# The start of a hybrid encoder layer: first weights on another queue, the first block of x in two transfers, norm_w turned in between, three fillers fewer

## The chip, the cores and the metric

The kernel runs on one core of a Trainium2 chip. Its time is that of the device in microseconds. Three runs of the kernel before took 625.95, 626.0 and 626.17 us; the median is 626.0. The engines are named as in the profile: PE is TensorE (PEld its weight loads), ACT is ScalarE, DVE is VectorE, POOL is GpSimd, SP is SyncE, which here only issues transfers.

## The reference

One layer of a bidirectional encoder on 512 tokens of width 2048, all float32:

```
h     = rms_norm(x, norm_w)                       # norm_w has 2048 gains
proj  = h @ w_in                                  # w_in: 2048 x 4608
q, k, v, g_attn, xr, g_lru = split(proj)
attn  = softmax attention of q, k, v (8 heads, 2 for k and v, rope, q and k normed)
lru   = convolution of xr, then a gated linear recurrence forwards and backwards
mixed = [rms_norm(attn) * silu(g_attn), rms_norm(lru) * silu(g_lru)]
out   = x + mixed @ w_out                         # w_out: 2048 x 2048
```

## The kernel before

Nearly all of its time is matmul work on PE. Each float32 operand is split into a high part, rounded to the matmul's own 32-bit format, and a low part, what is left; a product is three matmuls: high by high, high by low and low by high (lines 153 to 155). The pieces are 128 x 128 against 128 x 512.

**The start.** The first product is x times the columns of w_in that make xr, from column C_XR = 2560, 512 columns at a time, accumulated over 16 row blocks of 128 (8 chunks of two). It needs x turned, features on partitions and tokens along the free axis. So for each block of 128 features four 128 x 128 tiles, one for each 128 tokens, are transposed by PE (`xturn`, line 258) into one PSUM bank. ScalarE scales the bank by that block's column of norm_w and writes the high part (line 263); VectorE writes the low part (line 266). norm_w itself arrives as 16 rows of 128 (the tile nw_st) and is also turned by PE, in `columns` (line 194), and copied to SBUF by VectorE (line 196). The weights arrive in the tile wr; for the first chunk VectorE casts the high part (line 223) and subtracts for the low part (line 224); later ScalarE casts. The first real matmul, of `proj_feat` at line 394, needs the high part of x's first block and of the first weights. The order on PE at that place is: high by high for the four pieces of the first weights, then the turns of x's second block, then the low parts.

**Fillers.** `busy(n)` (line 1167) issues n matmuls of a tile of ones into a bank that nobody reads. WARM = 12 of them stand ahead of everything on PE, WARM2 = 5 behind the turns of the first block.

**What sets the order.** At the start PE, ScalarE, VectorE and SyncE run in the order in which the code is written; each engine is in order, and waits on semaphores. A transfer is issued by SyncE's or ScalarE's queue and bumps one of eight completion semaphores, taken in turn over both queues (DMAHW0 to DMAHW7 in the order below); a transfer whose semaphore is still in use first waits for that earlier transfer. Before: norm_w goes out on ScalarE's queue, ahead of its table load (line 1184); SyncE issues x's first 128 features (256 KB, all tokens), the first 128 rows of weights (256 KB), x's second 128 features, the second weights, and then chunks of 512 KB, at lines 245 and 211.

**The last stage.** The output product reads blocks of w_out through `feed1` and `feed2`. In `feed2` the two halves of a block are fetched as one transfer, but for the second half of the columns (g = 1) and i < 3 as two (line 1004).

Of the kernel before, what the change touches and what calls it, by code (L numbers as in the profile page):

```python
# [11 lines left out]
F32 = mybir.dt.float32  # L12
# [5 lines left out]
P = 128  # L18
SEQ = 512
DM = 2048  # L20
KT = DM // P
NT = SEQ // P
# [17 lines left out]
SOON = 150  # L40


WARM, WARM2 = 12, 5


BEGIN, STEPS, LATE = 11, 2, 3
# [10 lines left out]
C_Q, C_K, C_GA, C_XR, C_GL = 0, 1024, 1536, 2560, 3584  # L57
# [6 lines left out]
def hybrid_kernel(  # L64
# [20 lines left out]
    nc = tc.nc  # L85
    xf = x.rearrange("b s d -> (b s) d")
# [5 lines left out]
    def opened(name, side):  # L92
        pools[name] = tc.alloc_tile_pool(name=name, bufs=1, side=side, reuse_waits="tile")
        order[side].append(name)
        return pools[name]
# [9 lines left out]
    wring = opened("wr", "left").ring(3 * 4096, name="wring")  # L105
# [12 lines left out]
    def nm(s):  # L118
        cnt[0] += 1
        return f"{s}_{cnt[0]}"  # L120

    def x2():
        return pools["xw"].tile([P, SEQ], F32R, tag="x2", bufs=32, name=nm("x2"))
# [4 lines left out]
    def b4(dt=F32, shape=(P, 2, SEQ)):  # L128
        return pools["lru"].tile(list(shape), dt, tag="b4", bufs=LRU_B4, name=nm("b4"))
# [13 lines left out]
    def mm():  # L143
        return ps.tile([P, SEQ], F32, tag="mm", name=nm("mm"))

    def const(shape, name, dt=F32):
        return cp.tile(list(shape), dt, tag=name, name=name)

    def f(ap):
        return ap.bitcast(F32)  # L150
# [21 lines left out]
    nw_st = const([KT, P], "nw_st")  # L172
# [14 lines left out]
    nw = const([P, KT], "nw")  # L187
    vec = const([P, R_END], "vec")

    def columns(dst, src):  # L190

        n = src.shape[0]
        pt = mm()
        nc.tensor.transpose(pt[:, :n], src, ident[:n, :n])  # L194
        with tc.high_priority():
            nc.vector.tensor_copy(dst, pt[:, :n])
# [6 lines left out]
    loads_done = {}  # L203

    def wraw(w, r0, c0, nk=1, queue=nc.sync):

        raw = wring.tile([P, 2, SEQ], F32, name=nm("wr"))
        src = w[r0 : r0 + 2 * P, c0 : c0 + SEQ].rearrange("(k p) e -> p k e", p=P)
        for k in range(nk):
            ks = slice(k * 2 // nk, (k + 1) * 2 // nk)  # L210
            loads_done[queue] = queue.dma_start(raw[:, ks, :], src[:, ks, :]).ins
            yield raw
# [3 lines left out]
    def wsplit(raw, k, copy=nc.scalar.copy):  # L216

        turn_of[0] += k
        pool = pools["wx" if "wx" in pools and turn_of[0] % 2 else "xw"]
        hi = pool.tile([P, SEQ], F32R, tag="wh", bufs=4, name=nm("wh"))  # L220
        lo = pool.tile([P, SEQ], F32R, tag="wl", bufs=4, name=nm("wl"))
        done = (
            copy(hi, raw[:, k, :]).ins,  # L223
            nc.vector.tensor_sub(lo, raw[:, k, :], f(hi)).ins,  # L224
        )
        split_done[-1] = split_done[turn_of[0] - k] = done
        return hi, lo
# [11 lines left out]
    def xload(c, nk=1):  # L239

        xc = b4(shape=(P, NT, 2 * P))
        for k in range(nk):
            ks = slice(k * 2 * P // nk, (k + 1) * 2 * P // nk)
            cs = slice(c * 2 * P + ks.start, c * 2 * P + ks.stop)
            nc.sync.dma_start(xc[:, :, ks], xf[:, cs].rearrange("(t p) d -> p t d", p=P))
            yield xc

    def behind(those):
        stack = ExitStack()
        for ins in those:  # L250
            stack.enter_context(tc.issue_after(ins))
        return stack

    def xturn(xc, kk, then=None):
        pt = mm()
        for t in range(NT):
            ks = slice(kk % 2 * P, (kk % 2 + 1) * P)
            nc.tensor.transpose(pt[:, t * P : (t + 1) * P], xc[:, t, ks], ident)  # L258
        if then:
            then()  # L260
        xh[kk], xl[kk] = x2(), x2()
        with behind(split_done[-1] if kk > 3 else ()):
            highs[kk // 2] = nc.scalar.activation(
                xh[kk], pt, AF.Identity, scale=nw[:, kk : kk + 1]
            ).ins
        nc.vector.scalar_tensor_tensor(
            xl[kk], pt, nw[:, kk : kk + 1], f(xh[kk]), op0=ALU.mult, op1=ALU.subtract
        )
# [39 lines left out]
    def xchunk(c):  # L308
# [3 lines left out]
        if c < TURNED:  # L312
            with tc.high_priority(AHEAD):
                for k in range(2):
                    xturn(xc, 2 * c + k)
            if c == 2:
                yield
            with behind(split_done[2][1:] if c == 2 else ()):
                xsquare(xc, c)
            yield  # L320
            return
# [555 lines left out]
    def split(*blocks):  # L877

        i = split_of[0] % 4
        split_of[0] += 1  # L880
        hi, lo = (
            pools["out" if i else "fin"].tile([P, 2, SEQ], F32R, tag=f"{t}{i}", bufs=1, name=nm(t))
            for t in ("wh", "wl")
        )
        n = 0
        for b in blocks:
            to = slice(n, n + b.shape[1])
            nc.scalar.copy(hi[:, to], b)  # L888
            nc.vector.tensor_sub(lo[:, to], b, f(hi[:, to]))  # L889
            n += b.shape[1]  # L890
        return hi, lo
# [9 lines left out]
    def block(m, k, c, n=1):  # L901

        return w_out[(2 * m + k) * P : (2 * m + k + 1) * P, c * SEQ : (c + n) * SEQ]
# [41 lines left out]
    def in_wr(n=2):  # L945
        return wring.tile([P, n, SEQ], F32, name=nm("wr"))

    def in_av(n=2):
        return aring.tile([P, n, SEQ], F32, name=nm("wr"))
# [48 lines left out]
    def feed2(g, i, got):  # L998

        m = mixed[i][0] // (2 * P)  # L1000
        x_ = in_wr()
        if g and i < 3:
            for j in range(2):
                nc.sync.dma_start(x_[:, j], block(m, 1, 2 * g + j))
        else:
            nc.sync.dma_start(x_.rearrange("p j e -> p (j e)"), block(m, 1, 2 * g, 2))
        if g == 0:
            z = in_av(1)
            nc.sync.dma_start(z[:, 0], t4[m])
        else:  # L1010
            z = kept_t2.pop(i)
            nc.vector.tensor_add(z, z, x_[:, 1:2])
        yield
        got.append(split(x_))
        yield
        got.append(split(z))
        yield

    def outputs(work):
# [6 lines left out]
        for g, n, i in order:  # L1026
            parts.append([])
            feeds.append((feed1, feed2)[n](g, i, parts[-1]))
# [136 lines left out]
    def busy(n):  # L1165
        for _ in range(n):
            nc.tensor.matmul(warm[:, : 2 * P], wv[:, :P], wv, start=True, stop=True)  # L1167
# [8 lines left out]
    )  # L1176
    given = {}
    with tc.high_priority():
        xs, ws = xload(0, 2), wraw(w_in, 0, C_XR, 2)
        nc.scalar.dma_start(nw_st, norm_w.rearrange("(k p) -> k p", p=P))  # L1180
        xc, raw = next(xs), next(ws)
        next(xs), next(ws)
        table = const([P, 1], "table")
        nc.scalar.activation(table, ones[:, :1], AF.Exp)
        first = []

        def split_first():
            first.append(wsplit(raw, 0, nc.vector.tensor_copy))

        columns(nw, nw_st)  # L1190
        xturn(xc, 0, split_first)
        busy(WARM2)
    stats = xstats()
# [29 lines left out]
    for step in proj_feat(C_XR, a1, first, given):  # L1223
        if step is None:
            with tc.high_priority():
                first.append(wsplit(raw, 1, nc.vector.tensor_copy))
                xturn(xc, 1)
            xsquare(xc, 0)
            move(None)
            given[1] = wload(w_in, 2 * P, C_XR)  # L1230
            continue
        c, e = step
        move(step)
        if (c, e) == (1, 2):
            s2.close()
        if (c, e) == (4, 2):
            with tc.high_priority(AHEAD):
                vec_load()
        if (c, e) == (7, 1):
            columns(vec, vec_st)  # L1240
        if (c, e) in ((4, 3), (KT // 2 - 1, 0)):
            with tc.high_priority(AHEAD), tc.issue_after(split_done[-1][1]):
                next(stats)
# [216 lines left out]
```

## Time and profile before

| | |
|---|---|
| median of three runs | 626.0 us (625.95 to 626.17) |
| the profiled execution | 626.48 us |
| its span, first to last instruction | 624.7 us |
| PE busy | 620.0 us, 99% of the span |
| DVE busy | 495.3 us, 79% |
| ACT busy | 352.4 us, 56% |
| POOL busy | 101.8 us, 16% |
| moved by transfers | 127.61 MB, 204 GB/s on average |

All times below are from the start of the span. Busy time of PE is modelled as overlapping: a matmul's length reaches over the start of the next one, so its rate is read from the distance of starts. The time around the span, 626.48 - 624.7 = 1.78 us, is not in the trace.

### The profile page before, as it was taken

How to read it: one execution, taken by the hardware profiler on the slowest of the kernel's cores; microseconds unless marked ns; L12 is line 12 of the kernel's file. 1: busy time of each engine (PE TensorE's matmuls, PEld its weight loads, DVE VectorE, ACT ScalarE, POOL GpSimd, SP SyncE). 2: the span in 40 equal slices, each digit the busy share in tenths (PEclk: the TensorE clock that was granted, in tenths of full speed). 3: DMA queues.
4: the chain of work that ended last, by engine and by line, in shares of the span. 5: the costliest groups of instructions: out<-in, count | busy, mean ns of one | idle time of the engine just before them, and what ended most of it. 6: DMA issues, size and time to landing. Idle time of an engine off the chain costs nothing.

```text
span 624.7 us, 8293 instructions
## 1 busy us (share of the span) xinstructions
PE 620.0 (99%) x2756; PEld 512.6 (82%) x2756; DVE 495.3 (79%) x800; ACT 352.4 (56%) x617; POOL 101.8 (16%) x135
## 2 busy tenths in 40 slices
PE   9999999999999999999999999999999999999997
PEld 7888888888888888888888888888888888888886
DVE  5958979986699876887887888549979866887776
ACT  3675799479946833545485548338345633443441
POOL 0000210112003622622123223100210101010010
PEclk9999999999999999999999999999999999999999
DMA  8878686759774599479659646932995777897252
GB/s 285 277 210 271 178 202 171 175 135 195 239 235 137 170 247 240 100 204 270 192 173 258 201 137 192 256 91 76 283 254 184 216 250 242 288 333 230 68 202 101
DMA packets 74026, 127.61 MB, mean 204 GB/s; under 512 B 6664, under 2 KB 29312, under 8 KB 73984
## 3 DMA queue, kind: packets, MB, share of 16 engines
q1 hardware_dynamic: 66096, 109.65, 56.7%
q0 software_dynamic: 7712, 17.31, 14.3%
q8 instruction: 21, 0.34, 0.2%
q14 instruction: 21, 0.17, 0.1%
q10 hardware_dynamic: 176, 0.14, 0.1%
HBM read 110.29 MB, written 37.75 MB: 237 GB/s over the span
## 4 chain that ended last, share of the span: by engine, by line
PE 99%; DVE 0%; issue 0%
PE pj L154 20%; PE pj L155 20%; PE pj L153 20%; PE mm L1040 14%; PE pj L1040 11%; PE mm L155 4%; PE mm L154 3%; PE mm L153 3%; PE pj L394 2%; PE mm L258 1%; PE mm L1167 1%; PE mm L836 0%; DVE cb L1069 0%; PE mm L194 0%; PE mm L373 0%; DVE ones L159 0%
## 5 line engine op out<-in xcount | busy, mean ns | idle before, releaser
L153 PE MATMUL pj<-x,wh 128*128 128x512 f32 x368 | 143.5, 390 | 0.0
L155 PE MATMUL pj<-x,wl 128*128 128x512 f32 x368 | 143.2, 389 | 0.0
L154 PE MATMUL pj<-x,wh 128*128 128x512 f32 x368 | 143.2, 389 | 0.0
L223 ACT CAST wh<-wr 128x512 fp32r<-128x512 f32 x142 | 84.5, 618 | 81.5 <-PE pj L154 29.8
L224 DVE TENSOR_TENSOR wl<-wr,wh 128x512 fp32r<-128x512 f32 x144 | 98.5, 712 | 20.5 <-ACT wh L223 19.2
L888 ACT CAST wh<-wr 128x1024 fp32r<-128x1024 f32 (+1 forms) x72 | 60.6, 860 | 75.3 <-PE mm L1040 36.0
L889 DVE TENSOR_TENSOR wl<-wr,wh 128x1024 fp32r<-128x1024 f32 (+1 forms) x72 | 68.6, 983 | 29.0 <-ACT wh L888 28.9
L153 PEld LDWEIGHTS pj<-x,wh 128*128 128x128 f32 x368 | 69.1, 188 | 14.4
L154 PEld LDWEIGHTS pj<-x,wh 128*128 128x128 f32 x368 | 69.1, 188 | 14.3
L155 PEld LDWEIGHTS pj<-x,wl 128*128 128x128 f32 x368 | 69.1, 188 | 14.3
L154 PE MATMUL pj<-wl,x 128*128 128x512 f32 x192 | 74.7, 389 | 0.0
L155 PE MATMUL pj<-wh,x 128*128 128x512 f32 x192 | 74.7, 389 | 0.0
L153 PE MATMUL pj<-wh,x 128*128 128x512 f32 x192 | 74.7, 389 | 0.0
L912 POOL DMA_DIRECT2D t<-in_w_out_dram x40 | 33.6, 907 | 156.0 <-DMA t<-in_w_out_dram 96.9
L1040 PE MATMUL mm<-wh,ml 128*128 128x512 f32 x126 | 49.0, 389 | 0.0
L1040 PE MATMUL mm<-wh,mh 128*128 128x512 f32 x126 | 49.0, 389 | 0.0
L1040 PE MATMUL mm<-wl,mh 128*128 128x512 f32 x126 | 49.0, 389 | 0.0
L153 PEld LDWEIGHTS pj<-wh,x 128*128 128x128 f32 x192 | 36.0, 188 | 7.6
L154 PEld LDWEIGHTS pj<-wl,x 128*128 128x128 f32 x192 | 36.0, 188 | 7.5
L155 PEld LDWEIGHTS pj<-wh,x 128*128 128x128 f32 x192 | 36.0, 188 | 7.4
L712 POOL TENSOR_SCALAR p<-p,sm 128x512 f32<-128x512 f32 x32 | 24.2, 761 | 89.4 <-DVE sm L711 89.4
L1040 PE MATMUL pj<-wl,mh 128*128 128x512 f32 (+1 forms) x100 | 38.5, 385 | 0.0
(205 smaller groups left out, 1052.9 us busy)
## 6 DMA issues: line engine op xcount, KB each, us to landing
wr<-in_w_in_dram SPq DMA_DIRECT2D x71, 512.0 KB, 5.0
wr<-in_w_out_dram SPq DMA_DIRECT2D x21, 512.0 KB, 5.1
t<-in_w_out_dram POOLq DMA_DIRECT2D x40, 256.0 KB, 7.1
wr<-t SPq DMA_DIRECT2D x40, 256.0 KB, 5.8
pd<-u SPq DMA_DIRECT2D x16, 512.0 KB, 3.0
pt<-pd SPq DMA_DIRECT2D x64, 128.0 KB, 4.1
t<-in_w_out_dram SPq DMA_DIRECT2D x24, 256.0 KB, 5.3
wr<-in_w_out_dram SPq DMA_DIRECT2D x22, 256.0 KB, 4.2
```

Source lines behind the costliest of these rows:

```text
L153: nc.tensor.matmul(acc, lh, rh, start=start, stop=False)
L154: nc.tensor.matmul(acc, lh, rl, start=False, stop=False)
L155: nc.tensor.matmul(acc, ll, rh, start=False, stop=stop)
L223: copy(hi, raw[:, k, :]).ins,
L224: nc.vector.tensor_sub(lo, raw[:, k, :], f(hi)).ins,
L258: nc.tensor.transpose(pt[:, t * P : (t + 1) * P], xc[:, t, ks], ident)
L394: nc.tensor.matmul(acc[e], w[:, e * P : (e + 1) * P], x_[2 * c + k], start=c == k == j == 0, stop=False,)
L712: last_pool[0] = nc.gpsimd.tensor_scalar(p, p, sm, 0.0, op0=ALU.mult, op1=ALU.add).ins
L888: nc.scalar.copy(hi[:, to], b)
L889: nc.vector.tensor_sub(lo[:, to], b, f(hi[:, to]))
L912: nc.gpsimd.dma_start(dst, src, accum_op=ALU.add)
L1040: nc.tensor.matmul(dst[s][:, es], lh[:, ts_], rh[:, es], start=i == ends_[0] and j == 0, stop=i == ends_[1] and j == 2,)
```

## The change

Five edits, four of them in the first 6 us:

- The first weights (256 KB) go out on ScalarE's queue, ahead of norm_w. SyncE issues x's first 128 features as two transfers of 128 KB, tokens 0 to 255 and 256 to 511, then x's second 128 features and the second weights.
- PE turns the first two token tiles of x, then norm_w, then the other two, instead of norm_w first.
- WARM goes from 12 to 11.
- WARM2 goes from 5 to 3.
- In `feed2` only i < 2 keeps two transfers, so one pair in the last stage becomes one transfer.

```diff
-WARM, WARM2 = 12, 5
+WARM, WARM2 = 11, 3
@@ xturn
         for t in range(NT):
+            if kk == 0 and t == 2:
+                columns(nw, nw_st)
             ks = slice(kk % 2 * P, (kk % 2 + 1) * P)
             nc.tensor.transpose(pt[:, t * P : (t + 1) * P], xc[:, t, ks], ident)
@@ feed2
-        if g and i < 3:
+        if g and i < 2:
@@ the start
     with tc.high_priority():
-        xs, ws = xload(0, 2), wraw(w_in, 0, C_XR, 2)
+        raw = wring.tile([P, 2, SEQ], F32, name=nm("wr"))
+        xc = b4(shape=(P, NT, 2 * P))
+        ws = w_in[: 2 * P, C_XR : C_XR + SEQ].rearrange("(k p) e -> p k e", p=P)
+        xs = xf[:, : 2 * P].rearrange("(t p) d -> p t d", p=P)
+        nc.scalar.dma_start(raw[:, 0], ws[:, 0])
+        for ts_ in (slice(0, 2), slice(2, 4)):
+            nc.sync.dma_start(xc[:, ts_, :P], xs[:, ts_, :P])
         nc.scalar.dma_start(nw_st, norm_w.rearrange("(k p) -> k p", p=P))
-        xc, raw = next(xs), next(ws)
-        next(xs), next(ws)
+        nc.sync.dma_start(xc[:, :, P:], xs[:, :, P:])
+        loads_done[nc.sync] = nc.sync.dma_start(raw[:, 1], ws[:, 1]).ins
         table = const([P, 1], "table")
         nc.scalar.activation(table, ones[:, :1], AF.Exp)
...
-        columns(nw, nw_st)
         xturn(xc, 0, split_first)
         busy(WARM2)
```

On PE, from the last filler of the first group to the first ones of the second, the order before (b is the block of x, nw_st the rows of norm_w, mm a PSUM bank; in brackets what a row waits for):

```order
L1167 MATMUL mm_115<-ones 128x256
L194 MATMUL mm_144<-ident,nw_st 128x16 [waits DMAHW0_49,Pool_49]
L258 MATMUL mm_147<-ident,b_2_136 128x128 [waits DMAHW1_49]
L258 MATMUL mm_147<-ident,b_2_136 128x128 x3
L1167 LDWEIGHTS ones
L1167 MATMUL mm_115<-ones 128x256
```

And now:

```order
L1169 MATMUL mm_115<-ones 128x256
L260 MATMUL mm_144<-ident,b_3_135 128x128 [waits DMAHW1_49,Pool_49]
L260 MATMUL mm_144<-ident,b_3_135 128x128
L194 MATMUL mm_147<-ident,nw_st 128x16 [waits DMAHW3_49]
L260 MATMUL mm_144<-ident,b_3_135 128x128 [waits DMAHW2_49]
L260 MATMUL mm_144<-ident,b_3_135 128x128
L1169 LDWEIGHTS ones
L1169 MATMUL mm_115<-ones 128x256
```

The turn of norm_w stands between the second and third turn of x, and three transfers are waited for in turn where there were two.

On SP, the head of the queue before (b is x, wr the weights; the 4x256 and 2x512 rows are the next chunks):

```order
L245 DMA b_2_136<-in_x_dram 128x4x128
L211 DMA wr_138<-in_w_in_dram 128x512
L245 DMA b_2_136<-in_x_dram 128x4x128
L211 DMA wr_138<-in_w_in_dram 128x512
L245 DMA b_19_190<-in_x_dram 128x4x256
L211 DMA wr_192<-in_w_in_dram 128x2x512
L245 DMA b_31_250<-in_x_dram 128x4x256
L245 DMA b_38_282<-in_x_dram 128x4x256 [waits DMAHW0_49]
```

And now:

```order
L1187 DMA b_3_135<-in_x_dram 128x2x128 x2
L1189 DMA b_3_135<-in_x_dram 128x4x128
L1190 DMA wr_134<-in_w_in_dram 128x512
L245 DMA b_19_188<-in_x_dram 128x4x256
L211 DMA wr_190<-in_w_in_dram 128x2x512
L245 DMA b_31_248<-in_x_dram 128x4x256 [waits DMAHW0_49]
L245 DMA b_38_280<-in_x_dram 128x4x256 [waits DMAHW1_49]
```

Four issues still stand ahead of the chunks, and chunk 2 of x (b_31) now waits for DMAHW0, which is the first weights' semaphore; before, chunk 3 was the first to wait, for norm_w's.

On ACT, the first rows now, where before the transfer of norm_w (L1180) stood alone ahead of the table load:

```order
L1185 DMA wr_134<-in_w_in_dram 128x512
L1188 DMA nw_st<-in_norm_w_dram 16x128
L1192 ACT_TABLE_LOAD
L1192 ACTIVATE table<-ones 128x1 [waits DVE_49]
L265 ACTIVATE x_8_156<-mm_144,nw 128x512 [waits DVE_49,PE_49]
```

The table load has moved behind one more issue.

## Prediction, made before the changed kernel was run

> **What bounds the kernel now.** I read the page first, then the windows and the waits of TensorE, then the timeline of the start.
>
> ```profile
> span 624.7 us, 8293 instructions
> PE 620.0 (99%) x2756; PEld 512.6 (82%) x2756; DVE 495.3 (79%) x800; ACT 352.4 (56%) x617; POOL 101.8 (16%) x135
> PE 99%; DVE 0%; issue 0%
> ```
>
> The chain that ended last is TensorE from end to end. The windows say where its missing 4.7 us lie (columns: window, its length, PE busy with count, granted clock, DMA share, GB/s).
>
> ```profile
> 0.00:6.00 6.00, 4.96 (x23) 1.00 0.58 181
> 6.00:621.00 615.00, 615.00 (x2735) 1.00 0.72 205
> 621.00:624.70 3.70, 0.05 (x1) 0.95 0.42 142
> ```
>
> From 6 to 621 us TensorE is busy in every microsecond, and the last 3.7 us are the tail, which the change doesn't touch. So the change can pay only at the start: by how much earlier the unbroken row of matmuls begins, and at which speed its first ones run. The waits of PE's weight loads, over the whole span, agree:
>
> ```profile
> PEld L1167 <- DVE ones L159: 1.0, 1, 1.0
> PEld mm L194 <- issue: 0.4, 1, 0.4
> PEld mm L155 <- DVE q L658: 0.3, 1, 0.3
> PEld pj L394 <- ACT x L263: 0.2, 1, 0.2
> ```
>
> Now the start, in order of time (start, duration, engine, line):
>
> ```profile
> 1.04 2.74 PE L1167 MATMUL mm<-ones 128*128 128x256 bf16 x12 [1.04 <-DVE ones L159]
> 3.71 0.18 PEld L194 LDWEIGHTS mm<-ident,nw_st 16*128 16x128 f32 x1 [0.41 <-issue]
> 3.92 0.71 PEld L258 LDWEIGHTS mm<-ident,b 128*128 128x128 f32 x4
> 3.93 1.11 PE L258 MATMUL mm<-ident,b 128*128 128x128 f32 x4
> 4.03 0.17 DVE L196 COPY nw<-mm 128x16 f32<-128x16 f32 x1 [3.05 <-PE mm L194]
> 4.62 1.00 PEld L1167 LDWEIGHTS <-ones 128*128 128x128 bf16 x5
> 4.83 1.27 PE L1167 MATMUL mm<-ones 128*128 128x256 bf16 x5
> 4.99 0.43 DVE L223 CAST wh<-wr 128x512 fp32r<-128x512 f32 x1 [0.78 <-DMA wr<-in_w_in_dram]
> 5.08 0.69 ACT L263 ACTIVATE x<-mm,nw 128x512 fp32r<-128x512 f32 x1 [2.38 <-PE mm L258]
> 5.82 1.09 PEld L394 LDWEIGHTS pj<-x,wh 128*128 128x128 f32 x4 [0.19 <-ACT x L263]
> 5.82 1.51 PE L394 MATMUL pj<-x,wh 128*128 128x512 f32 x4
> 6.94 0.59 PEld L258 LDWEIGHTS mm<-ident,b 128*128 128x128 f32 x4
> 7.17 0.60 PE L258 MATMUL mm<-ident,b 128*128 128x128 f32 x4
> 7.52 1.17 PE L394 MATMUL pj<-x,wl 128*128 128x512 f32 x4
> ```
>
> Twelve fillers, the turn of norm_w (L194), four turns of x (L258), five fillers. The four turns end at 3.93 + 1.11 = 5.04; ScalarE makes the high half of x from 5.08 to 5.77; at 5.82 the first real matmul starts. The weights' high half is ready at 4.99 + 0.43 = 5.42, 0.40 us before that: the path runs through the turns, not the weights. The five fillers' weight loads end at 5.62; PE then sits 0.19 us until ScalarE is done.
>
> Two speeds are in these rows. Four turns took 1.11 us at 3.93 and 0.60 at 7.17; four L394 matmuls 1.51 and then 1.17. TensorE works at about half rate up to some point between 5.82 and 7.17, though the clock column says 1.00. I take 6.4.
>
> **The change, part by part.** The transfers (first their issue, start and length; then, in the last three rows, size and time from issue to landing, each asked for around one issue alone):
>
> ```profile
> 0.72 0.45 ACTq L1180 DMA_DIRECT2D nw_st<-in_norm_w_dram  x1
> 0.72 0.43 SPq L245 DMA_DIRECT2D b<-in_x_dram  x1
> 1.20 1.28 ACT L1184 ACT_TABLE_LOAD   x1 [1.20 <-PEq L1445]
> 1.21 0.49 SPq L211 DMA_DIRECT2D wr<-in_w_in_dram  x1
> 2.22 0.51 SPq L211 DMA_DIRECT2D wr<-in_w_in_dram  x1
> 3.80 1.10 SPq L245 DMA_DIRECT2D b<-in_x_dram  x2
> 4.95 1.43 SPq L211 DMA_DIRECT2D wr<-in_w_in_dram  x1
> b<-in_x_dram SPq DMA_DIRECT2D x1, 256.0 KB, 2.9
> wr<-in_w_in_dram SPq DMA_DIRECT2D x1, 256.0 KB, 3.8
> b<-in_x_dram SPq DMA_DIRECT2D x1, 512.0 KB, 6.3
> ```
>
> So x's first columns land at 0.72 + 2.9 = 3.62 and the first weights at 1.21 + 3.8 = 5.0. x was there 0.31 us before its turn at 3.93: the fillers and L194 ahead of it set that start.
>
> *One filler fewer ahead of the turns.* Twelve fillers took 2.74 us, five 1.27: (2.74 - 1.27) / 7 = 0.21 us each. The first turn can start at 3.71 - 0.21 = 3.50, in the place where L194 stood. The sequence then is the same five turns, with norm_w third: 0.21 us earlier all along, if every transfer is there. That is the most that this edit can give: the first real matmul at 5.61.
>
> *Is the data there?* Bounds from the rows. First half of x: issued at 0.72, half the size of the one that took 2.9, with the weights beside it: lands between about 3.2 and 3.6; first turn at 3.5 to 3.65. norm_w: it moves behind the weights' issue, so about 0.49 us, to 1.2. Its turn ran at 3.71, so it had landed in 2.99 us at most: by 4.2 now, later if the weights ahead of it in its queue hold it up. Second half of x: issued second on SyncE, at 1.2; with the 2.9 of the whole that is 4.1. At the pace of now (four turns of x from 3.93 to the filler at 4.83: 0.225 each) norm_w is wanted at 3.95 and the second half at 4.17. The later bound is the first rival below, 4.5. I take the last two turns 0.1 to 0.2 us earlier than now, nearer to the early end, since the 2.9 was measured for twice the bytes. PE is in order: behind the turn of norm_w stand two turns, three fillers and every matmul, so a late norm_w costs one for one.
>
> *What the gain is worth.* An earlier start by 0.1 to 0.2 us is spent at half rate if the faster rate still comes at 6.4: half of it, 0.05 to 0.1. If the faster rate moves along, all of it. I take 0.1 us.
>
> *Two fillers fewer behind the turns.* 2 x 0.21 = 0.42 us, all of it inside the wait for ScalarE (0.69 us from the turns' end): nothing by itself. PE's pause ahead of the first real matmul grows from 0.19 to about 0.6 us. Price only through the speed (rival).
>
> *First weights in ScalarE's queue.* Earlier by up to 0.49 us, with 0.40 us to spare now: no gain. ScalarE's table load starts 0.49 us later and its table is ready near 3.2 instead of 2.70; it is needed at 4.87. SyncE still issues four transfers first, with x's second block and the second weights third and fourth as before. PE needs that block at 6.94, without idle; it would need it at 6.8 now.
>
> *A wait added.* The transfer of chunk 2 of x (one of two at 3.80) now waits for the first weights, as the completion semaphores go round by eight; behind it in SyncE's queue are chunk 3 and the next weights. It may go out up to 1.2 us later (5.0). What hides it is the backlog: the block issued at 2.78 takes 6.3 us to land, and the issue at 4.95 took 1.43 instead of 0.5. Without that backlog it would be the full 1.2. I take zero.
>
> *One transfer instead of two in the last stage.*
>
> ```profile
> 568.63 6.24 SPq L1004 DMA_DIRECT2D wr<-in_w_out_dram  x6
> 591.14 1.06 ACT L888 CAST wh<-wr 128x1024 fp32r<-128x1024 f32 x1 [2.10 <-PE mm L1040]
> DMA to landing us min/median/max: 3.6/3.9/4.4
> ```
>
> The pair that is joined is the last of the six, issued by 574.9 and landed by 579.3; its first reader starts at 591.14. Nothing, with 11 us of cover.
>
> The sum: -0.1 (bounds -0.21, and +0.17 with the data at 4.5). The profiled execution took 626.48 us, a span of 624.7 and 1.78 around it; it would come to 626.4. The median of the three runs is 626.0, so 625.9.
>
> **The Trainium skill against these rows.** "DMA: Bandwidth & Descriptors", section "Issuing engines are not separate DMA queues", says that transfers issued by several engines share the same 16 DMA engines and save the issue time alone. It speaks against any gain from the weights' new queue, and fits the first rival; by it alone the change would come to 626.2. The rows here can't settle it, since only 8 KB went through ScalarE's queue.
>
> **The rivals.** Two more rows, the second from the DMA view of 0 to 7 us in 40 slices:
>
> ```profile
> 8.53 2.00 PE L394 MATMUL pj<-x,wh 128*128 128x512 f32 x8
> GB/s 0 0 0 0 0 0 0 0 0 0 61 152 170 205 278 363 310 340 357 366 301 185 219 263 298 325 357 293 263 249 170 167 208 231 187 219 240 281 275 287
> ```
>
> *1. x's second half shares the pipe with the weights.* The 512 KB of both, issued at 0.72 and 1.21, were through at 5.0. With both starting at 0.72, and neither favoured, x's second half and norm_w land up to 0.49 us sooner than that: 4.5. Then the third turn starts at 4.55 and the fourth at 4.78; now they start at 4.38 and 4.61 (3.93 and two or three steps of 0.225). The first real matmul is as much later, 0.17 us: 626.2. If they land as late as the weights do now, at 5.0, it is 0.6 to 0.65: 626.6. For it: the weights come in 2 KB rows and x in 512 B ones. Against: the pipe moved only 61 to 205 GB/s in its first 0.7 us. It decides when the third turn starts after 4.38. Chance 0.16.
>
> *2. The faster rate comes a spell later: slower.* It came some 5.4 us after the first filler, at 6.4, with no pause of PEld above 0.41 us. Now there is a pause of about 0.6 us ahead of the first real matmul, and perhaps one at norm_w. If such a pause starts the count anew at 5.6, the rate comes at 11.0; 4.6 us at half rate cost 2.3, less 0.1: 628.2. Against: pauses of 0.41 and 0.19 us did no harm. Chance 0.09. In the Trainium skill's "TensorE: Matmul & The Clock Gate", Part 1, the gate opens after a busy window of about 3.4 us; a window lost that way would cost an estimated 1.7 us, 627.6.
>
> *3. The faster rate comes before the first real matmul.* Then the four L394 take 1.0 us from start to start (7.52 to the next four at 8.53) instead of 1.35 (5.82 to 7.17): 0.35, and with the full 0.2 of the earlier start 625.45. If it comes already among the turns (1.11 us down to 0.60), up to 0.5 more: 624.9. Nothing in the change brings it, so where the rate opens would have to vary from run to run. The three runs lie within 0.22 us (625.95 to 626.17), which speaks against much of that. Chance 0.11. The same page of the Trainium skill calls the window free-running, so by it this rival and its opposite would both be met among the runs.
>
> **How the numbers follow.** Forecast 0.64 (625.8 to 626.0), rival 1 0.16, rival 2 0.09, rival 3 0.11. The range takes in the forecast, rival 1 to its end at 626.6 and rival 3 to halfway between its two values, 625.2; it leaves rival 2 out. A measurement here tells about 0.2% from no change, 1.25 us: only rival 2 goes past it, so slower is 0.09; faster would need every gain above twice over, 0.02; no change 0.89.
>
> **What would show it.** Right: first turn near 3.5, turns over by 4.85 to 4.95, first L394 between 5.6 and 5.75, the four turns of the next block again near 0.6 us, and PE full from 6 to 621. Rival 1: PEld waits on a DMA at the third turn. Rival 2: the turns near 7 still take 1.1 us. Wrong altogether: an idle PE after 6 us, say at the block that SyncE now sends later.

## The result, and the profile after

The change made the kernel slower. Its median is 628.56 us over 6 runs (628.2 to 629.24), against 626.09 for the kernel before over 6 runs beside it (625.89 to 626.6); the ratio is 1.004, with a 95% interval of 1.0027 to 1.0053. The forecast was 625.9, no change. The profiled execution took 628.47 us, 1.99 more than that of before, and its span, 626.6, is 1.9 longer. The medians are 2.47 apart; the traces account for 1.9 of that, mostly since the profiled run of before was itself 0.4 us above its median.

The page's head and the waits of PE's weight loads, over the whole span:

```profile
span 626.6 us, 8285 instructions
PE 620.7 (99%) x2753; PEld 512.7 (82%) x2753; DVE 495.0 (79%) x800; ACT 352.5 (56%) x617; POOL 101.6 (16%) x135
PEld mm L260 <- issue: 1.7, 2, 1.5
PEld L1169 <- DVE ones L159: 1.0, 1, 1.0
PEld pj L396 <- ACT x L265: 0.6, 1, 0.6
PEld mm L194 <- issue: 0.3, 1, 0.3
PEld mm L155 <- DVE q L660: 0.3, 1, 0.3
```

New is the first row, a pause of 1.5 us ahead of a turn of x; the wait for ScalarE grew from 0.2 to 0.6, as the prediction said. The windows show where the 1.9 us are (columns as in the prediction):

```profile
0.00:6.00 6.00, 3.91 (x17) 1.00 0.68 178
6.00:623.00 617.00, 616.77 (x2738) 1.00 0.72 204
623.00:626.60 3.60, 0.00 (x0) 1.00 0.43 146
```

In the first 6 us PE is busy for 3.91 us where it was 4.96. From 6 us on it is as full as before, and the tail is as long. So it is the start alone, here in the timeline (lines 260, 396 are 258, 394 of before):

```profile
1.04 2.53 PE L1169 MATMUL mm<-ones 128*128 128x256 bf16 x11 [1.04 <-DVE ones L159]
4.58 0.28 PEld L260 LDWEIGHTS mm<-ident,b 128*128 128x128 f32 x2 [1.49 <-issue]
4.62 0.66 PE L260 MATMUL mm<-ident,b 128*128 128x128 f32 x2 [1.04 <-DMA b<-in_x_dram]
5.20 0.28 PE L194 MATMUL mm<-ident,nw_st 16*128 16x16 f32 x1
5.42 0.69 PE L260 MATMUL mm<-ident,b 128*128 128x128 f32 x2
6.14 0.69 ACT L265 ACTIVATE x<-mm,nw 128x512 fp32r<-128x512 f32 x1 [2.99 <-PE mm L260]
6.88 2.08 PE L396 MATMUL pj<-x,wh 128*128 128x512 f32 x4
8.76 0.95 PE L260 MATMUL mm<-ident,b 128*128 128x128 f32 x4
9.46 1.16 PE L396 MATMUL pj<-x,wl 128*128 128x512 f32 x4
```

Two losses add up, from start to start. The first real matmul is at 6.88 instead of 5.82: 1.06. The four that begin there and the four turns behind them still run at the low rate: 6.88 to 8.76 is 1.88 instead of 1.35, and 8.76 to 9.46 is 0.70 instead of 0.35. Together 1.06 + 0.53 + 0.35 = 1.94, the whole difference of the spans.

The chain of what ended last names the first loss (start, length, what):

```profile
0.73 3.75 DMA b<-in_x_dram
4.48 0.14 issue
4.62 0.66 PE mm L260 x2
```

The first half of x, 128 KB, landed 3.75 us after its issue, at 4.48; before, the whole 256 KB had taken 2.9. The DMA view of 0 to 7 us in 40 slices, after:

```profile
DMA  0000000000999336699999999999956698999999
GB/s 0 0 0 0 0 0 0 0 0 0 117 94 82 70 123 178 243 342 363 340 357 299 334 328 345 351 328 287 240 179 205 228 287 287 310 316 351 351 351 369
```

In the first three busy slices the 16 engines are occupied nine tenths and more and move 117, 94 and 82 GB/s; before, the same slices rise from 61 to 170 and the next three to 363.

The packets say which rows came first. From 1.7 to 2.5 us, the change (queue, packets, MB, share of the time of the 16 engines; q1 is SyncE's queue, q10 ScalarE's):

```profile
q10 hardware_dynamic: 34, 0.07, 91.4%
```

And before:

```profile
q1 hardware_dynamic: 213, 0.11, 48.0%
q10 hardware_dynamic: 22, 0.01, 6.3%
```

In these 0.8 us the change moved 34 packets of weights and none of x, although both had been issued at 0.72 to 0.73; before, x's queue had moved 213. The 34 packets kept the engines busy for an estimated 0.34 us each (91.4% of 0.8 us on 16 engines). Why these first rows of weights were that slow no run shows.

### The profile page after: what moved, and what is told of

Its sections match the earlier page's. It is cut to its first block, busy times and chain, and to the rows that moved or that the text cites. A ratio compares the mean times of both kernels' runs of the same rounds, so it can differ in the third digit from the quotient of the medians.

```text
span 626.6 us, 8285 instructions
## 1 busy us (share of the span) xinstructions
PE 620.7 (99%) x2753; PEld 512.7 (82%) x2753; DVE 495.0 (79%) x800; ACT 352.5 (56%) x617; POOL 101.6 (16%) x135
## 4 chain that ended last, share of the span: by engine, by line
PE 99%; DMA 1%; ACT 0%; DVE 0%; issue 0%
PE pj L154 20%; PE pj L155 20%; PE pj L153 20%; PE mm L1042 14%; PE pj L1042 11%; PE mm L155 3%; PE mm L154 3%; PE mm L153 3%; PE pj L396 2%; PE mm L260 1%; DMA b<-in_x_dram 1%; ACT x L265 0%; PE mm L838 0%; DVE cb L1071 0%; PE mm L194 0%
```

## The experiments

Theory A, after the result: the weights, which now reach the pipe (the 16 DMA engines) first, make x and norm_w late, and PE's idle time makes the faster matmul rate late on top. Theory B: the fillers taken away are the cause. The kernel before ran beside each; its medians there were 626.2 to 626.35. In the code, `...` marks lines left out.

**The weights' queue alone.**

```diff
...
+        nc.scalar.dma_start(raw[:, 0], ws[:, 0])
         nc.scalar.dma_start(nw_st, norm_w.rearrange("(k p) -> k p", p=P))
...
+        nc.sync.dma_start(xc[:, :, :P], xs[:, :, :P])
...
```

> The kernel before with one edit: the first weights go out on ScalarE's queue ahead of norm_w, x's first columns stay one transfer on SyncE's queue, fillers stay 12 and 5, norm_w is turned first. Theory A (the weights beside x make x late, and the pause that follows makes the faster matmul rate late): x's first columns and norm_w land near 4.7 instead of 3.62, the first turn is after 4.6, the first real matmul near 6.9, the faster rate after 9; 628.3. Theory B (the fillers taken away are the cause): with 12 and 5 back nothing is lost; 626.1, at most 626.5.

Measured: 629.01 us, ratio 1.0043 (1.0031 to 1.0055), all five runs between 628.5 and 629.9. Its waits and its timeline:

```profile
PEld mm L194 <- issue: 2.4, 1, 2.4
5.73 0.26 PE L194 MATMUL mm<-ident,nw_st 16*128 16x16 f32 x1 [1.95 <-DMA nw_st<-in_norm_w_dram]
7.81 2.08 PE L394 MATMUL pj<-x,wh 128*128 128x512 f32 x4
9.69 1.05 PE L258 MATMUL mm<-ident,b 128*128 128x128 f32 x4
```

Theory B falls: with all 17 fillers the loss is as large. x landed 4.7 us after its issue and norm_w 4.4. The two halves of x in the change probably softened this, since two turns could start before the rest was there: the first real matmul is at 7.81 here and at 6.88 in the change.

**The same queue, behind norm_w.** The two issues of ScalarE's queue in the kernel just shown (q_alone in the expectation) are exchanged.

```diff
-        nc.scalar.dma_start(raw[:, 0], ws[:, 0])
         nc.scalar.dma_start(nw_st, norm_w.rearrange("(k p) -> k p", p=P))
+        nc.scalar.dma_start(raw[:, 0], ws[:, 0])
```

> q_alone with the two issues of ScalarE's queue changed about: norm_w first, the first weights behind it, so that these go out 0.5 us after x's first columns. If the second queue as such starves x (both share the pipe, x's 512 B rows against 2 KB rows): x's first columns still land after 4.3, the first real matmul is after 6.5, 627.5 or more. If what counts is that the weights reach the pipe first: x lands by 3.8, the first real matmul is at 5.7 to 6.0, 625.9 to 626.4.

Measured: 626.53, ratio 0.9999 (0.9990 to 1.0007). First matmul and landing of x (3.0 us after the issue) are where they were, and the DMA view of 0 to 7 us rises as it did:

```profile
b<-in_x_dram SPq DMA_DIRECT2D x1, 256.0 KB, 3.0
wr<-in_w_in_dram ACTq DMA_DIRECT2D x1, 256.0 KB, 4.0
GB/s 0 0 0 0 0 0 0 0 0 0 50 164 152 164 264 339 345 337 339 284 304 298 363 354 325 348 360 325 351 304 357 339 369 351 357 392 374 369 351 421
5.82 1.60 PE L394 MATMUL pj<-x,wh 128*128 128x512 f32 x4
```

So a second queue as such neither cost nor brought anything here. What cost was that the weights were issued together with x, and not half a microsecond behind it. In this kernel x's queue moved 191 packets from 1.7 to 2.5 us; with the weights first it moved one.

**The change without the queue.** This is the changed kernel with another order of issues. x in two transfers, norm_w's turn in between and 11 and 3 fillers stay; the first weights go out third on SyncE's queue.

```diff
-        nc.scalar.dma_start(raw[:, 0], ws[:, 0])
+        nc.scalar.dma_start(nw_st, norm_w.rearrange("(k p) -> k p", p=P))
         for ts_ in (slice(0, 2), slice(2, 4)):
             nc.sync.dma_start(xc[:, ts_, :P], xs[:, ts_, :P])
-        nc.scalar.dma_start(nw_st, norm_w.rearrange("(k p) -> k p", p=P))
+        nc.sync.dma_start(raw[:, 0], ws[:, 0])
```

> The changed kernel with the first weights back on SyncE's queue, third behind the two halves of x, and norm_w alone on ScalarE's; the two halves, the turn of norm_w in between and 11 and 3 fillers stay. Theory A (the weights' place is the cause): the first half lands by 3.5, the last turn ends by 5.0, first real matmul 5.6 to 5.8: 625.9 to 626.2. If the two transfers or the turn in between are the cause: a pause of a microsecond at the turns is still there and the time stays above 627.5.

Measured: 626.78, ratio 1.0011 (1.0003 to 1.0020); six of eleven runs between 626.1 and 626.8, five between 627.6 and 628.2. In the profiled one (626.39) the turns begin at 3.37, earlier than forecast:

```profile
3.37 0.63 PE L260 MATMUL mm<-ident,b 128*128 128x128 f32 x2
5.76 1.17 PE L396 MATMUL pj<-x,wh 128*128 128x512 f32 x4 [0.29 <-DVE wh L223]
```

Neither the two transfers nor the turn in between delays the turns. The first real matmul, at 5.76, now waits for the weights' high half, since the weights go third. The gap between the two groups of runs is what the next kernels are about.

**The fillers alone.**

```diff
-WARM, WARM2 = 12, 5
+WARM, WARM2 = 11, 3
```

> The kernel before with 11 and 3 fillers instead of 12 and 5 and nothing else. Theory A: x is there at 3.62, norm_w's turn starts at 3.5, the pause ahead of the first real matmul grows to 0.6 us and does no harm; first real matmul at 5.6 to 5.8, 625.9 to 626.1. Theory B: the pause puts off the faster rate by some 3 us; 627.5 to 628.

Measured: 626.55, ratio 1.0011 (1.0001 to 1.0020). Again two groups: seven of twelve runs from 625.7 to 626.6, five from 627.3 to 628.5, while none of the 29 runs of the kernel before beside it went over 627.2. Neither expectation covers it alone: with the pause of 0.6 us some runs lose nothing and others about 1.5 us (the medians of the two groups are 626.44 and 627.99).

**Two fillers fewer behind the turns, nothing else** (the kernel before with `WARM, WARM2 = 12, 3`).

> The kernel before with 12 and 3 fillers: the turns stay where they are, only the pause ahead of the first real matmul grows from 0.19 to 0.6 us. If that pause makes the faster rate late in some runs (as the spread of the runs with 11 and 3 fillers, 625.7 to 628.5, suggests): a third to a half of the runs near 628, the others near 626.1. If that spread was noise or came from the filler ahead: all within 625.6 to 627.2 like the kernel before.

Measured: 626.42, ratio 1.0001 (0.9992 to 1.0010): three of twelve runs over 627.3, two of 35 of the kernel before. Three of twelve alone is too few to tell from that; it goes the way of the five of twelve and five of eleven above. The trace fell on one of the three (628.2), and shows what the late rate costs by itself:

```profile
span 626.4 us, 8289 instructions
5.82 2.08 PE L394 MATMUL pj<-x,wh 128*128 128x512 f32 x4
7.69 1.06 PE L258 MATMUL mm<-ident,b 128*128 128x128 f32 x4
```

The first real matmul is at 5.82, to the hundredth where it was before, and nothing waits after it; yet the span is 1.7 us longer, because the four matmuls, the turns and the four matmuls behind them run at the low rate (2.08, 1.06 and 2.05, against 1.51, 0.60 and 1.17).

**A pause ahead of the turns, with the data on time** (the kernel before with `WARM, WARM2 = 5, 5`).

> The kernel before with 5 and 5 fillers: TensorE stands idle from about 2.1 us to norm_w's turn at 3.1, and to x's turns at 3.65; every transfer as before. If a pause ahead of the turns is what puts the faster rate off: the first real matmul comes early, at 5.5, and still the rate comes after 8, 627.0 to 628.3. If only the lateness of the data costs: 625.8.

Measured: 627.14, ratio 1.0010 (1.0002 to 1.0019), all eleven runs from 626.6 to 627.8. The trace fell on the lowest:

```profile
3.27 0.26 PE L194 MATMUL mm<-ident,nw_st 16*128 16x16 f32 x1 [0.98 <-DMA nw_st<-in_norm_w_dram]
5.60 1.78 PE L394 MATMUL pj<-x,wh 128*128 128x512 f32 x4
```

The first real matmul is 0.22 us earlier than before in this trace, and the median is 0.8 longer: a pause of 1.4 us costs an estimated 1 us, with the data as early as in the kernel before.

**The changed kernel with the pauses filled** (`WARM, WARM2 = 17, 5` for 11, 3).

> The changed kernel with 17 and 5 fillers instead of 11 and 3, so that the 1.5 us in which TensorE stood idle ahead of the first turn are filled. If the late rate comes from that pause: first real matmul still near 6.9, but the faster rate at 6.4 to 6.6, so the loss shrinks from 2.5 us to about the 1.06 us of lateness less what then runs at full rate, 0.4: 626.6 to 627.0. If the lateness alone is the cause and the rate comes when it comes: 628.5 as the changed kernel.

Measured: 626.88, ratio 1.0010 (1.0001 to 1.0019), eleven runs from 626.5 to 627.5. Its start:

```profile
4.64 0.65 PE L260 MATMUL mm<-ident,b 128*128 128x128 f32 x2
6.90 1.20 PE L396 MATMUL pj<-x,wh 128*128 128x512 f32 x4 [0.23 <-ACT x L265]
7.94 0.60 PE L260 MATMUL mm<-ident,b 128*128 128x128 f32 x4
```

The turns and the first real matmul are as late as in the change, and the first turns as slow (0.65 us for two, 0.66 there), but the first real matmul and the turns behind it run at the full rate. Six fillers ahead and two behind bring the loss from 2.47 us down to 0.66 (626.88 - 626.22); what is left is the lateness, less what now runs faster.

**Only the second pause filled** (the changed kernel with 11 and 7).

> The changed kernel with 11 and 7 fillers: the pause ahead of the first real matmul is filled, the 1.5 us ahead of the turns stay idle. If the pause ahead of the turns puts off the faster rate: still late, above 627.8 in nearly every run. If it is the pause ahead of the first real matmul that matters most: near 626.9, like the changed kernel with 17 and 5.

Measured: 628.53, ratio 1.003 (1.0019 to 1.0042). Little or nothing is won: the idle time ahead of the turns is enough to make the rate late. It is no clean test of the second pause, since the seven fillers, themselves at the low rate, put the first real matmul of the trace off to 7.33.

**The halves of x on two queues.** This too is the changed kernel with another order of issues: the second half of x, then norm_w on ScalarE's queue; the first weights second on SyncE's; 11 and 6 fillers.

```diff
-WARM, WARM2 = 11, 3
+WARM, WARM2 = 11, 6
...
-        nc.scalar.dma_start(raw[:, 0], ws[:, 0])
-        for ts_ in (slice(0, 2), slice(2, 4)):
-            nc.sync.dma_start(xc[:, ts_, :P], xs[:, ts_, :P])
+        nc.sync.dma_start(xc[:, :2, :P], xs[:, :2, :P])
+        nc.scalar.dma_start(xc[:, 2:, :P], xs[:, 2:, :P])
         nc.scalar.dma_start(nw_st, norm_w.rearrange("(k p) -> k p", p=P))
+        nc.sync.dma_start(raw[:, 0], ws[:, 0])
```

> The changed kernel's order of turns, but the second queue carries the second half of x's first columns (then norm_w) and the first weights are second on SyncE's queue; 11 and 6 fillers. If it was the weights' rows reaching the pipe first that held up x: both halves land by 3.5, turns from 3.5, last turn ends by 4.9, first real matmul near 5.6, 626.0 to 626.4. If two queues that start together slow each other whatever they carry: first half after 3.9, first real matmul after 6.1, 626.6 or more.

Measured: 626.31, ratio 0.9997 (0.9987 to 1.0007). The first turns are in time, so two queues that start together need not slow x (here both began with x's 512 B rows); but norm_w, now behind x's half, is late, and the turns behind it stand:

```profile
3.50 0.66 PE L260 MATMUL mm<-ident,b 128*128 128x128 f32 x2
4.63 0.23 PE L194 MATMUL mm<-ident,nw_st 16*128 16x16 f32 x1 [0.47 <-DMA nw_st<-in_norm_w_dram]
6.00 1.19 PE L396 MATMUL pj<-x,wh 128*128 128x512 f32 x4
```

The first real matmul came at 6.00, not at 5.6: that part of the expectation was wrong.

**Earlier turns and more fillers** (the kernel before with `WARM, WARM2 = 11, 6`, nothing else).

> The kernel before with 11 and 6 fillers: the turns 0.21 us earlier as with 11 and 3, but the pause ahead of the first real matmul filled. If the pause is what costs: no run near 628, the median 0.1 to 0.2 us below the kernel before, 625.9 to 626.1. If the earlier turns cost something of their own: the spread of 11 and 3 fillers stays.

Measured: 626.67, ratio 1.0005 (0.9996 to 1.0013); ten of the eleven runs from 626.1 to 627.8, and one at 1276.93, about twice the others, which I can't explain and which the ratio leaves out. The gain didn't come, and the trace says where it went:

```profile
5.39 1.20 PE L394 MATMUL pj<-x,wh 128*128 128x512 f32 x4
PEld pj L153 <- ACT wh L223: 0.7, 1, 0.7
PEld pj L155 <- DVE wl L224: 0.6, 1, 0.6
40.09 1.34 ACT L343 ACTIVATE xu<-xu,nw 128x512 f32<-128x512 f32 x2 [3.82 <-DMA xu<-xd]
```

The matmuls began 0.43 us earlier, and at the full rate; then PE stood 1.3 us for the weights of a later chunk, both waits between 42 and 45 us. ScalarE cast these weights late because ahead of the cast it waited 3.82 us for a block of x that is fetched back (xu), until 40.09. In the kernel before PE has no wait there; it comes to that chunk's second low half just after it is done, at 43.69 (42.41 and 1.28) against 44.22 (there ScalarE had that block at 39.31):

```profile
42.41 1.28 DVE L224 TENSOR_TENSOR wl<-wr,wh 128x512 fp32r<-128x512 f32 x2
44.22 0.39 PE L155 MATMUL pj<-x,wl 128*128 128x512 f32 x1
```

**One filler more** (the kernel before with `WARM, WARM2 = 12, 6`).

> The kernel before with a sixth filler behind the turns, so that PE doesn't stop ahead of the first real matmul. If that pause of 0.19 us is why some runs of the kernel before are near 627 to 628: no run above 626.8, the median 626.1 to 626.3. If those runs are something else: the same spread as the kernel before beside it, and the median 0 to 0.05 us above it.

Measured: 626.7, ratio 1.0001 (0.9991 to 1.0011), runs from 625.8 to 627.5. The first expectation failed: four of twelve runs lie above 626.8. The median, 0.35 above that of the kernel before, doesn't fit the second either, though the interval takes in no change. The trace fell on the fastest run (625.76), and it shows something else:

```profile
3.93 0.79 PE L258 MATMUL mm<-ident,b 128*128 128x128 f32 x4
5.49 1.20 PE L394 MATMUL pj<-x,wh 128*128 128x512 f32 x4
```

Up to 3.93 us everything is as in the kernel before, and yet the four turns took 0.79 us instead of 1.11: the faster rate came among them, an estimated 2 us earlier. PE waited for nothing from 6 to 60 us, not even near 43, where ScalarE had its block of x at 38.71.

**The last stage alone** (`i < 2` in `feed2`).

> The kernel before with the edit of the last stage alone (one transfer instead of two for the third block). All theories: its reader comes 11 us after it lands, so nothing: 626.0 to 626.5, ratio 1.000. If the joined transfer or the semaphores that go round otherwise from there on cost something, an idle PE after 575 us and over 626.9.

Measured: 626.43, ratio 0.9999 (0.9990 to 1.0008), as all theories had it. Its start is that of the kernel before, and in its trace too the rate came early, behind the turns:

```profile
3.93 0.95 PE L258 MATMUL mm<-ident,b 128*128 128x128 f32 x4
5.66 1.21 PE L394 MATMUL pj<-x,wh 128*128 128x512 f32 x4 [0.23 <-ACT x L263]
```

Near 43 us PE then stood 0.8 us for the weights of the later chunk, and the run took 626.66. No version's median was clearly below that of the kernel before.

## Why the prediction was wrong

*What bounds the kernel.* Right: PE was full from 6 us to the tail in both traces, and the start alone decided.

*Is the data there?* This is the step that failed. It took the first half of x to land at 3.2 to 3.6 because it is half of the bytes that took 2.9 us, and named the weights beside it without a price of their own. It landed at 4.48. The 2.9 us of x's transfer was the wrong row to scale: the weights' first rows went ahead of it, 34 packets in 0.8 us with none of x, and in that time the pipe moved a third and less of its later rate. The queue alone cost 2.8 us, and the same queue half a microsecond later nothing. x's second half (4.1 in the prediction) landed at 5.0, 3.8 us after its issue, and norm_w (4.2) at 4.7.

*First weights in ScalarE's queue: no gain.* The sign of the gain was right, but the step weighed only what the weights win and left out what x loses to them, except in the first rival. That rival had sharing, with neither favoured, and the loss on the second half alone: 0.17 us with the data at 4.5, 0.6 to 0.65 with them at 5.0. The second half did land at 5.0. What the rival left out is that the weights went first and the first half waited too: the first turn was at 4.62 and the first real matmul 1.06 later, beyond its outer bound of 0.65. "DMA: Bandwidth & Descriptors" of the Trainium skill, section "Issuing engines are not separate DMA queues", has transfers of several issuing engines interleave on the same 16 engines. The trace agrees from 2.5 us on (43 packets of ScalarE's queue and 27 of SyncE's up to 3.0), and not in the 0.8 us before. The section also has the second queue save the issue time alone; the queue that cost and brought nothing behind norm_w (0.9999) agrees.

*One filler fewer, the earliest start.* Right where the data is there: with the fillers alone the first real matmul was at 5.61, as worked out.

*Two fillers fewer: price only through the speed.* Right that they are hidden, and right that the pause is 0.6 us; the chance that the pause makes the rate late was too small. With data on time some of the runs paid (five of twelve, five of eleven; three of twelve in the run that the kernel before nearly matches), and in the change all six did, where PE had stood 1.5 us already.

*Rival 2.* Given 0.09 and 628.2; the time was 628.56. It came about, but behind the late data, not behind the fillers' removal: with all 17 fillers the new queue cost as much, and filled pauses brought the time back to 626.88. That 628.2 lies so near is luck: the rival had 2.3 us of half rate and no lateness, and of the 1.94 us in the two traces 1.06 are lateness and 0.88 rate. The prediction took the two rivals as alternatives, each with its own chance. They are one chain: late data make PE idle, idle PE keeps the low rate.

*Rival 3.* The change didn't meet it. But its condition, that the rate opens at another place from run to run, does hold: with the same work up to 3.93 us it came near 6.4 in the profiled run before, and during or just behind the turns in the traces of 12 and 6 fillers and of the last stage alone (four turns in 1.11, 0.79 and 0.95 us). That the three runs lay within 0.22 us spoke less against it than the prediction thought. "TensorE: Matmul & The Clock Gate" of the Trainium skill, Part 1, has the rate open after a busy window of about 3.4 us that runs freely. These traces agree that it opens at no fixed place; the length of the window no run here shows. The two groups in which the runs with 11 and 3 fillers fall lie 1.4 to 1.6 us apart, near the estimated 1.7 of the prediction.

*The added wait of chunk 2 and the last stage.* Both at zero, as forecast: chunk 2 went out at 4.18 instead of 3.80 and no wait followed; the last stage alone gave 0.9999.

*A bound that was missing.* Even with the data on time a gain can be taken back near 43 us, by a chunk whose weights ScalarE casts behind a block of x that has to land first. Of the four traces in which the first real matmuls began at 5.39 to 5.66 at the full rate, three stood there for 0.8 to 1.3 us; the fourth (12 and 6 fillers), whose block landed earliest, did not. Why that landing moves from trace to trace is not shown.

Left open: which run of a kernel with a pause of 0.6 us keeps the low rate, and why the first rows of weights were slow. The clock column of the profile reads 1.00 at the start of the traces, so the low rate can't be read there.

## What to carry to other kernels

At the start of a kernel price a transfer by what is issued ahead of it or beside it on any queue, and let the bytes that the first instruction needs go out first: here the second queue brought nothing, and which rows came first decided 2.8 us. Do not treat a late transfer and a low matmul rate as two risks: what leaves TensorE idle in its first microseconds can be paid twice, so fillers should cover the time until the data really come, and no more. And before hoping for an earlier start, look for the next place where the stream of data, not the engine, sets the pace.

## What the runs showed of the hardware

With the weights first, the 16 DMA engines were counted busy nine tenths and more while moving 117, 94 and 82 GB/s in their first three slices of 0.175 us; with x first and the weights on the same second queue they moved 50, 164 and 152, at half the share and less, and 339 three slices later. Whether 256 KB of weights were issued together with 256 KB of x or half a microsecond behind them moved the landing of x from 4.7 to 3.0 us after its issue.

The faster matmul rate doesn't come at a fixed place: with the same work up to 3.93 us, four turns from there took 1.11, 0.95 and 0.79 us in three traces, and the first four real matmuls 1.51, 1.21 and 1.20. Idle time of 1.4 to 1.5 us ahead of the turns put it off further: to near 6.9 us in the fastest run with 5 and 5 fillers, where the data were on time, and to after 9 us in the change.
